# Row standard deviations of an 8192 x 8192 matrix: the last 2048 rows laid out 16 to a partition, and the first group loaded by one transfer

## Chip, cores and metric

The kernel runs on one core of a Trainium2 chip. The metric is the device time of an execution in microseconds (us); before the change its median over three runs is 651.74 us (651.38 to 651.85).

## What is computed

```
x: float32 [8192, 8192], normal random numbers
np.std(x, axis=1)        # float32 [8192]
```

For each row, the root of the mean square deviation from its mean. The input is 268 MB and is read once; the result is 32 KB.

## The kernel before

The 128 partitions P each hold rows of C = 8192 elements (32 KB). 30 groups (G) of 256 rows come first, two neighbouring rows to a partition (64 KB, 8.39 MB in a group), then four tail rows per partition (TR = 4, 4.19 MB each). Three buffers `buf` of one group each are used in turn.

**Loads.** SP issues every load (line 121), in order. Group 0 is loaded by eight transfers of 16 partitions each, `buf[0][k:P:8]` for k = 0 to 7 (lines 124 to 126); all eight increment one semaphore, which is why `landed` (line 108) counts seven more transfers for buffer 0. Groups 1 to 29 are one transfer of 128 partitions each; from group 3 on, SP first waits for the semaphore `free`, which PE's queue increments (line 200) when DVE and ACT are both done with the group that had the buffer. The four tail rows follow: two rows into buffer `xa`, the next in two halves into `xb`, and the last in eight pieces that get shorter (3072 down to 256 elements) into the rest of `xb`.

**Groups 0 to 28.** DVE sums both rows in one instruction (line 161, `s_all`). ACT squares and accumulates each row (line 167 in a loop, `q_all`). DVE turns them into N times the variance, `vN` (lines 250 to 252).

**Group 29 and the tail rows.** A row is split (`shared`, line 214): ACT takes its first 3072 elements with two passes (square, and copy, each with an accumulated sum), DVE takes the rest with `bn_stats` in pieces of 512 (line 206) and aggregates them (line 212). For group 29 DVE joins the two halves (lines 260 to 268); for tail rows POOL does (`joined`, line 227).

**Results.** `vN` is transposed by PE (line 275) so that each group's 256 results lie in one partition, ACT takes roots from PSUM (line 279, `std_g`) and SP stores them (line 282). Three of the tail rows are joined by POOL into `t3`, transposed by PE (line 303), rooted by ACT (line 314) and stored (line 316). The last row's pieces go through ACT, POOL and DVE into `tri`; DVE aggregates them into `fin` (line 318), transposes `fin` in blocks of 32 x 32 (line 320), ACT takes the root (line 322) and SP stores four partitions of 128 bytes (line 324). Then SP waits for the three stores.

The order on each engine is written out by hand; `Line.need` is a wait for another engine's count, `Line.did` an increment.

Of the kernel before, what the change touches and what calls it, by code (L numbers as in the profile page):

```python
# [7 lines left out]
FP32 = mybir.dt.float32  # L8
ACTF = mybir.ActivationFunctionType
# [6 lines left out]
def kernel(  # L16
# [7 lines left out]
    nc = tc.nc  # L24
    P = nc.NUM_PARTITIONS
    R, C = x.shape
    N = float(C)
# [2 lines left out]
    AX = mybir.AxisListType.X  # L30


    TR = 4
    G = (R // P - TR) // 2
    B0 = 2 * (G - 1)
    T0 = 2 * G * P
    xg = x[0:T0, :].rearrange("(g p j) m -> g p (j m)", g=G, p=P, j=2)
    xt_rows = x[T0:R, :].rearrange("(t p) m -> t p m", p=P)
    out_g = out[0:T0].rearrange("(g q) -> g q", q=2 * P)
    out_t = out[T0:R].rearrange("(t p) -> t p", p=P)  # L40

    out_l = out[T0:T0 + P].rearrange("(b i) -> b i", b=4)
    ACT_ROW = 3072
    N_D = float(C - ACT_ROW)
    H = C // 2
    pieces = [(3072, 768), (1536, 1024), (1024, 0), (1024, 512), (512, 0), (512, 0), (256, 0), (256, 0)]

    def sb(name, shape, dt=FP32):
        return ctx.enter_context(nc.sbuf_tensor(name, shape, dt))[:]

    def sem(name):
        return ctx.enter_context(nc.semaphore(name))

    NBUF = 3
    buf = [sb(f"x{i}", [P, 2 * C]) for i in range(NBUF)]

    dump = sb("dump", [P, C], mybir.dt.uint8)
    s_all = sb("s_all", [P, 2 * G + TR])
    q_all = sb("q_all", [P, 2 * G + TR])
    half = sb("half", [P, 2])  # L60
    agg = sb("agg", [P, 2 * G + TR - 1 - B0, 2])
    ident = sb("ident", [P, P])
    cinv = sb("cinv", [P, 1])
    nd = sb("nd", [P, 1])
    vN = sb("vN", [P, 2 * G])
    m2 = sb("m2", [P, 2 * G])
    u, w, uq, wq = (sb(n, [P, TR]) for n in ("u", "w", "uq", "wq"))
    t3 = sb("t3", [P, TR - 1])
    warm = sb("warm", [P, 1])

    fin = sb("fin", [P, 33])
    tr = sb("tr", [P, 32])
    std_l = sb("std_l", [P, 32])
    std_t = sb("std_t", [TR - 1, P])
    std_g = sb("std_g", [G, P, 2])
    n_act = sum(1 for _, a in pieces if a)
    n_bn = sum(-(-(n - a) // F) for n, a in pieces)
    tri = sb("tri", [P, 3 * n_act + n_bn * SD])
    q_p = sb("q_p", [P, n_act])
    m_p = sb("m_p", [P, n_act])  # L80
    bns = [sb(f"bn{i}", [P, (C - ACT_ROW) // F * SD]) for i in range(2)]
    ps_t = ctx.enter_context(nc.psum_tensor("ps_t", [TR - 1, P], FP32))[:]
    ps_g = ctx.enter_context(nc.psum_tensor("ps_g", [G, 2, P], FP32))[:]


    class Line:
# [11 lines left out]
    V = Line(nc.vector, "v")  # L98
    A = Line(nc.scalar, "a")
    Q = Line(nc.gpsimd, "q")  # L100
    T = Line(nc.tensor, "t")
    free, token, row_done, squared = sem("free"), sem("token"), sem("row_done"), sem("squared")
    lane = [sem(f"lane{i}") for i in range(NBUF)]
    NT = 4 + len(pieces)
    tail = [sem(f"tail{i}") for i in range(NT)]
    done_g, done_t, done_l = sem("done_g"), sem("done_t"), sem("done_l")

    def landed(g):
        return lane[g % NBUF], 16 * (g // NBUF + 1 + (P // 16 - 1) * (g % NBUF == 0))

    xl, xa, xb = (buf[k % NBUF] for k in (G - 1, G, G + 1))

# [7 lines left out]
    def load(dst, src, s):  # L120
        nc.sync.dma_start(out=dst, in_=src).then_inc(s, 16)  # L121


    S0 = P // 16
    for k in range(S0):
        load(buf[0][k:P:S0], xg[0][k:P:S0], lane[0])
    for g in range(1, G):
        if g >= NBUF:
            nc.sync.wait_ge(free, g - NBUF + 1)
        load(buf[g % NBUF], xg[g], lane[g % NBUF])  # L130
    nc.sync.wait_ge(free, G - NBUF + 1)
    for i, t in enumerate((1, 2)):
        load(xa[:, i * C:(i + 1) * C], xt_rows[t], tail[i])
    nc.sync.wait_ge(free, G - NBUF + 2)
    for h in range(2):
        load(xb[:, h * H:(h + 1) * H], xt_rows[3][:, h * H:(h + 1) * H], tail[2 + h])
    c0 = 0
    for i, (n, _) in enumerate(pieces):
        load(xb[:, C + c0:C + c0 + n], xt_rows[0][:, c0:c0 + n], tail[4 + i])
        c0 += n  # L140


    def q_op(op, *args, **kw):
        Q.need(Q, Q.n)
        return Q.did(op(*args, **kw))  # L145
# [6 lines left out]
    Q.did(nc.gpsimd.memset(nd, N_D))  # L152
    for j, a in enumerate(a for _, a in pieces if a):
        Q.did(nc.gpsimd.memset(tri[:, 3 * j:3 * j + 1], float(a)))
    Q.did(nc.gpsimd.memset(fin, 0.0))


    v_group = []
    for g in range(G - 1):
        nc.vector.wait_ge(*landed(g))  # L160
        v_group.append(V.did(nc.vector.reduce_sum(  # L161
            out=s_all[:, 2 * g:2 * g + 2],
            in_=buf[g % NBUF].rearrange("p (j m) -> p j m", j=2), axis=AX)))
# [39 lines left out]
    def bn_cols(bn, k, src):  # L203
        n = src.shape[1]
        for d0 in range(0, n, F):
            V.did(nc.vector.bn_stats(out=bn[:, k * SD:(k + 1) * SD], in_=src[:, d0:min(n, d0 + F)]))  # L206
            k += 1
        return k

    def aggregated(out_ap, bn):  # L210
        V.need(V, V.n)
        return V.did(nc.vector.bn_aggr(out=out_ap, in_=bn))  # L212

    def shared(r, parts):
        bn = bns[r % 2]
        k = 0
        for i, (src, arrived) in enumerate(parts):
# [6 lines left out]
            k = bn_cols(bn, k, src[:, a:src.shape[1]])  # L224
        aggregated(agg[:, r - B0, :], bn)

    def joined(out_ap, r0, r1):
        n = r1 - r0
        ndb = nd.to_broadcast((P, n))
        cb = cinv.to_broadcast((P, n))  # L230
        dm, dv = agg[:, r0 - B0:r1 - B0, 0], agg[:, r0 - B0:r1 - B0, 1]
        u_, w_ = uq[:, 0:n], wq[:, 0:n]
        q_op(nc.gpsimd.tensor_mul, u_, dm, dm)
        q_op(nc.gpsimd.tensor_add, u_, u_, dv)
        q_op(nc.gpsimd.tensor_mul, u_, u_, ndb)
        q_op(nc.gpsimd.tensor_add, u_, u_, q_all[:, r0:r1])
        q_op(nc.gpsimd.tensor_mul, w_, dm, ndb)
        q_op(nc.gpsimd.tensor_add, w_, w_, s_all[:, r0:r1])
        q_op(nc.gpsimd.tensor_mul, w_, w_, w_)
        q_op(nc.gpsimd.tensor_mul, w_, w_, cb)  # L240
        return q_op(nc.gpsimd.tensor_sub, out_ap, u_, w_)

    def v_op(op, *args, **kw):
        V.need(V, V.n)
        return V.did(op(*args, **kw))  # L245
# [3 lines left out]
    V.need(A, a_groups)  # L249
    v_op(nc.vector.scalar_tensor_tensor, out=m2[:, 0:B0], in0=s_all[:, 0:B0], scalar=1.0 / N,  # L250
         in1=s_all[:, 0:B0], op0=ALU.mult, op1=ALU.mult)
    v_op(nc.vector.tensor_sub, vN[:, 0:B0], q_all[:, 0:B0], m2[:, 0:B0])
    shared(B0, [(xl[:, 0:C], last)])
# [14 lines left out]
    v_groups = v_op(nc.vector.tensor_sub, vN[:, B0:2 * G], u_, w_)  # L268


    vg = vN.rearrange("p (g j) -> p g j", j=2)
    T.need(V, v_groups)
    T.need(Q, q_ident)
    for j in range(2):
# [3 lines left out]
    for j in range(2):  # L278
        a_std = A.did(nc.scalar.activation(out=std_g[:, :, j], in_=ps_g[:, j, :], func=ACTF.Sqrt,  # L279
                                           scale=1.0 / N))  # L280
    nc.sync.wait_ge(A.sem, a_std)
    nc.sync.dma_start(out=out_g, in_=std_g.rearrange("g p j -> g (p j)")).then_inc(done_g, 16)

    r = 2 * G + 2
# [4 lines left out]
    c0, k, j = C, 0, 0  # L289
    for i, (n, a) in enumerate(pieces):  # L290
        src = xb[:, c0:c0 + n]
        if a:
            cnt, mean, m2v = (tri[:, 3 * j + e:3 * j + e + 1] for e in range(3))
            nc.scalar.wait_ge(tail[4 + i], 16)
            A.did(squash(src[:, 0:a], a, ACTF.Copy, mean, scale=1.0 / a))
            A.did(squash(src[:, 0:a], a, ACTF.Square, q_p[:, j:j + 1]))
            if j == 0:
                Q.need(V, v_blocks)
                Q.need(A, a_blocks)
                q_op(nc.gpsimd.tensor_add, s_all[:, r:r + 1], s_all[:, r:r + 1], half[:, 0:1])  # L300
                q_op(nc.gpsimd.tensor_add, q_all[:, r:r + 1], q_all[:, r:r + 1], half[:, 1:2])
                T.need(Q, joined(t3, 2 * G, r + 1))
                T.did(nc.tensor.transpose(ps_t, t3, ident))  # L303
            Q.need(A, A.n)
            q_op(nc.gpsimd.tensor_mul, m_p[:, j:j + 1], mean, mean)
            q_op(nc.gpsimd.tensor_mul, m_p[:, j:j + 1], m_p[:, j:j + 1], cnt)
            q_op(nc.gpsimd.tensor_sub, m2v, q_p[:, j:j + 1], m_p[:, j:j + 1])
            j += 1
        nc.vector.wait_ge(tail[4 + i], 16)
        k = bn_cols(tri[:, 3 * n_act:], k, src[:, a:n])  # L310
        c0 += n

    A.need(T, T.n)
    a_std = A.did(nc.scalar.activation(out=std_t, in_=ps_t, func=ACTF.Sqrt, scale=1.0 / N))  # L314
    nc.sync.wait_ge(A.sem, a_std)
    nc.sync.dma_start(out=out_t[1:TR], in_=std_t).then_inc(done_t, 16)
    V.need(Q, Q.n)
    aggregated(fin[:, 0:2], tri)
    V.need(V, V.n)
    v_fin = V.did(nc.vector.transpose(out=tr, in_=fin[:, 1:33]))  # L320
    A.need(V, v_fin)
    A.did(nc.scalar.activation(out=std_l, in_=tr, func=ACTF.Sqrt))  # L322
    nc.sync.wait_ge(A.sem, A.n)
    nc.sync.dma_start(out=out_l, in_=std_l[0:P:32, :]).then_inc(done_l, 16)
    nc.sync.wait_ge(done_g, 16)
    nc.sync.wait_ge(done_t, 16)
    nc.sync.wait_ge(done_l, 16)


# [28 lines left out]
```

## Time and profile before

| what | value |
|---|---|
| profiled execution, time | 651.74 us |
| its span on the core | 649.7 us |
| DVE busy | 540.2 us (83% of the span) |
| ACT busy | 450.1 us (69%) |
| PE, POOL busy | 1.0 and 4.8 us |
| moved by DMA | 268.49 MB, 413 GB/s over the span |
| chain that ended last | DMA 62%, DVE 35%, SP's queue 1% |
| SP waits for `free`, in total | 586.3 us, 29 times |
| DVE line 161 waits for loads | 104.2 us, 29 times |

The page divides the span into 40 equal slices and gives for each the busy share of the engines in tenths, the mean busy share of the 16 transfer engines (DMA) and the rate in GB/s. A stage line gives a stretch of time, then each engine's busy time in it, the PE clock, the DMA share and the rate. The chain is followed back from the last instruction, at each step to what released it. In the timeline a row is start, duration, engine, line, operation, output <- input, and in brackets the idle time before it and what ended it. Times are us from the start of the span.

### The profile page before, as it was taken

How to read it: one execution, taken by the hardware profiler on the slowest of the kernel's cores; microseconds unless marked ns; L12 is line 12 of the kernel's file. 1: busy time of each engine (PE TensorE's matmuls, PEld its weight loads, DVE VectorE, ACT ScalarE, POOL GpSimd, SP SyncE). 2: the span in 40 equal slices, each digit the busy share in tenths (PEclk: the TensorE clock that was granted, in tenths of full speed). 3: DMA queues.
4: the chain of work that ended last, by engine and by line, in shares of the span. 5: the costliest groups of instructions: out<-in, count | busy, mean ns of one | idle time of the engine just before them, and what ended most of it. 6: DMA issues, size and time to landing. Idle time of an engine off the chain costs nothing.

```text
span 649.7 us, 684 instructions
## 1 busy us (share of the span) xinstructions
PE 1.0 (0%) x3; PEld 0.2 (0%) x3; DVE 540.2 (83%) x107; ACT 450.1 (69%) x158; POOL 4.8 (1%) x33
## 2 busy tenths in 40 slices
PE   0000000000000000000000000000000000000000
PEld 0000000000000000000000000000000000000000
DVE  0028988888998888998888898888898888899897
ACT  0026886666787666787666687666688666778786
POOL 0000000000000000000000000000000000000002
DMA  9999999999999999999999999999999999999996
GB/s 195 198 307 399 452 452 391 448 452 440 399 452 452 391 448 452 440 399 452 452 391 448 452 440 399 452 452 395 444 452 444 395 452 452 395 444 452 414 417 269
DMA packets 6221, 268.49 MB, mean 413 GB/s; under 512 B 810, under 2 KB 1099, under 8 KB 1739
## 3 DMA queue, kind: packets, MB, share of 16 engines
q1 hardware_dynamic: 6219, 268.47, 99.0%
q14 instruction: 2, 0.02, 0.0%
HBM read 268.44 MB, written 0.03 MB: 413 GB/s over the span
## 4 chain that ended last, share of the span: by engine, by line
DMA 62%; DVE 35%; SPq 1%; another core or an unknown queue 1%; issue 0%; PEldq 0%; ACT 0%; DVEq 0%; POOLq 0%
DMA x<-in_x_dram 62%; DVE s_all L161 29%; DVE bn L206 5%; DVE tri L206 1%; SPq L121 1%; DVE agg L212 0%; PEldq L200 0%; DVE fin L212 0%; DVE u L245 0%; ACT std_l L322 0%; DVE tr L320 0%; DVE w L245 0%; DVE vN L245 0%; DVE w L264 0%
## 5 line engine op out<-in xcount | busy, mean ns | idle before, releaser
L161 DVE TENSOR_REDUCE s_all<-x 128x2 f32<-128x16384 f32 x29 | 499.4, 17220 | 104.2 <-DMA x<-in_x_dram 104.2
L167 ACT ACTIVATE dump<-x 128x8192 uint8<-128x8192 f32 (+5 forms) x76 | 440.8, 5800 | 193.4 <-ACTq L175 169.3
L206 DVE BATCH_NORM_STATS2 bn<-x 128x6 f32<-128x512 f32 x50 | 30.0, 674 | 1.5 <-DMA x<-in_x_dram 1.5
L167 ACT ACTIVATION_READ_ACCUMULATOR dump<-x (+1 forms) x76 | 14.2, 186 | 0.0
L206 DVE BATCH_NORM_STATS2 tri<-x 128x6 f32<-128x512 f32 (+1 forms) x13 | 7.1, 614 | 0.0
L145 POOL TENSOR_TENSOR s_all<-s_all,half 128x1 f32<-128x1 f32 x1 | 0.2, 193 | 636.9 <-DVE agg L212 636.9
L212 DVE BATCH_NORM_AGGREGATE agg<-bn 128x2 f32<-128x60 f32 x5 | 2.1, 425 | 0.2
L171 ACT ACT_TABLE_LOAD x1 | 1.3, 1283 | 1.4 <-PEq L342 1.4
L322 ACT ACTIVATE std_l<-tr 128x32 f32<-128x32 f32 x1 | 0.2, 229 | 2.0 <-DVE tr L320 2.0
L275 PE MATMUL ps_g<-ident,vN 128*30 128x128 f32 x2 | 0.6, 407 | 626.0 <-DVE vN L245 626.0
L212 DVE BATCH_NORM_AGGREGATE fin<-tri 128x2 f32<-128x87 f32 x1 | 0.5, 547 | 0.1
L145 POOL TENSOR_TENSOR m_p<-tri 128x1 f32<-128x1 f32 x3 | 0.6, 194 | 1.4 <-ACT dump L167 1.3
L145 POOL TENSOR_TENSOR m_p<-m_p,tri 128x1 f32<-128x1 f32 x3 | 0.6, 192 | 0.2
L145 POOL TENSOR_TENSOR tri<-q_p,m_p 128x1 f32<-128x1 f32 x3 | 0.6, 192 | 0.2
L279 ACT ACTIVATE std_g<-ps_g 30x128 f32<-30x128 f32 x2 | 0.4, 258 | 0.0
L303 PE MATMUL ps_t<-ident,t 128*3 128x128 f32 x1 | 0.4, 375 | 15.1 <-POOL t L145 15.1
L275 PEld LDWEIGHTS ps_g<-ident,vN 128*30 128x30 f32 x2 | 0.1, 114 | 626.0 <-DVE vN L245 626.0
L245 DVE SCALAR_TENSOR_TENSOR m<-s_all 128x58 f32<-128x58 f32 x1 | 0.2, 220 | 0.1
L145 POOL TENSOR_SCALAR_AFFINE_SELECT ident<-ident 128x128 f32<-128x128 f32 x1 | 0.3, 294 | 0.1
L314 ACT ACTIVATE std_t<-ps_t 3x128 f32<-3x128 f32 x1 | 0.2, 250 | 0.0
L245 DVE TENSOR_TENSOR vN<-q_all,m 128x58 f32<-128x58 f32 x1 | 0.2, 220 | 0.0
L245 DVE TENSOR_TENSOR u<-agg 128x2 f32<-128x2 f32 x1 | 0.2, 160 | 0.1
(28 smaller groups left out, 4.4 us busy)
## 6 DMA issues: line engine op xcount, KB each, us to landing
x<-in_x_dram SPq DMA_DIRECT2D x2, 4096.0 KB, 35.7
x<-in_x_dram SPq DMA_DIRECT2D x2, 2048.0 KB, 28.6
x<-in_x_dram SPq DMA_DIRECT2D x1, 1536.0 KB, 34.0
x<-in_x_dram SPq DMA_DIRECT2D x2, 512.0 KB, 36.7
x<-in_x_dram SPq DMA_DIRECT2D x1, 768.0 KB, 35.5
x<-in_x_dram SPq DMA_DIRECT2D x37, 40.7
x<-in_x_dram SPq DMA_DIRECT2D x2, 256.0 KB, 37.4
x<-in_x_dram SPq DMA_DIRECT2D x2, 128.0 KB, 27.0
```

The source lines that it names most:

```text
L121: nc.sync.dma_start(out=dst, in_=src).then_inc(s, 16)
L145: return Q.did(op(*args, **kw))
L161: v_group.append(V.did(nc.vector.reduce_sum(out=s_all[:, 2 * g:2 * g + 2], in_=buf[g % NBUF].rearrange("p (j m) -> p j m", j=2), axis=AX)))
L167: return nc.scalar.activation(out=dump[:, 0:n], in_=src, func=func, scale=scale, accum_out=acc)
L171: A.did(nc.scalar.activation(out=warm, in_=warm, func=ACTF.Sqrt))
L206: V.did(nc.vector.bn_stats(out=bn[:, k * SD:(k + 1) * SD], in_=src[:, d0:min(n, d0 + F)]))
L212: return V.did(nc.vector.bn_aggr(out=out_ap, in_=bn))
L245: return V.did(op(*args, **kw))
L275: T.did(nc.tensor.transpose(ps_g[:, j, :], vg[:, :, j], ident))
L279: a_std = A.did(nc.scalar.activation(out=std_g[:, :, j], in_=ps_g[:, j, :], func=ACTF.Sqrt, scale=1.0 / N))
L303: T.did(nc.tensor.transpose(ps_t, t3, ident))
L314: a_std = A.did(nc.scalar.activation(out=std_t, in_=ps_t, func=ACTF.Sqrt, scale=1.0 / N))
```

## The change

The last 16 x 128 = 2048 rows are assigned to partitions differently: partition p gets the 16 neighbouring rows 6144 + 16p to 6144 + 16p + 15. The first 24 groups (GA) are as before. Groups 24 to 29 and the four tail rows are now columns of `xe`, the view of those 2048 rows with 16 rows to a partition: each group still has two neighbouring rows (64 KB) to a partition, but from one partition to the next it is 512 KB in x. The number, order and size of the transfers of groups 1 to 29 and of the tail stay.

The results of these 16 rows per partition are rooted in place into `std_e` (128 x 16) by three ACT instructions (12, 3 and 1 columns), and one store at the end writes 64 bytes of each partition. PE's transpose of the tail rows, DVE's transpose, two stores' buffers and the memset of `fin` go. PE's transposes for the groups have 24 columns instead of 30.

Group 0 is loaded by one transfer of 128 partitions, as the other groups are.

```diff
+    E = 16
     G = (R // P - TR) // 2
+    GA = (R // P - E) // 2
-    T0 = 2 * G * P
-    xg = x[0:T0, :].rearrange("(g p j) m -> g p (j m)", g=G, p=P, j=2)
-    xt_rows = x[T0:R, :].rearrange("(t p) m -> t p m", p=P)
+    T0 = 2 * GA * P
+    xg = x[0:T0, :].rearrange("(g p j) m -> g p (j m)", g=GA, p=P, j=2)
+    xe = x[T0:R, :].rearrange("(p e) m -> p (e m)", p=P)
+    xg = [xg[g] for g in range(GA)] + [xe[:, 2 * k * C:2 * (k + 1) * C] for k in range(G - GA)]
+    xt_rows = [xe[:, (E - TR + t) * C:(E - TR + t + 1) * C] for t in range(TR)]
...
-    S0 = P // 16
-    for k in range(S0):
-        load(buf[0][k:P:S0], xg[0][k:P:S0], lane[0])
-    for g in range(1, G):
+    for g in range(G):
...
-    Q.did(nc.gpsimd.memset(fin, 0.0))
...
+    A.did(nc.scalar.activation(out=std_e[:, 0:E - TR], in_=vN[:, 2 * GA:2 * G], func=ACTF.Sqrt,
+                               scale=1.0 / N))
...
-                T.need(Q, joined(t3, 2 * G, r + 1))
-                T.did(nc.tensor.transpose(ps_t, t3, ident))
+                q_t3 = joined(t3, 2 * G, r + 1)
...
-    A.need(T, T.n)
-    a_std = A.did(nc.scalar.activation(out=std_t, in_=ps_t, func=ACTF.Sqrt, scale=1.0 / N))
-    nc.sync.wait_ge(A.sem, a_std)
-    nc.sync.dma_start(out=out_t[1:TR], in_=std_t).then_inc(done_t, 16)
+    A.need(Q, q_t3)
+    A.did(nc.scalar.activation(out=std_e[:, E - TR:E - 1], in_=t3, func=ACTF.Sqrt, scale=1.0 / N))
     V.need(Q, Q.n)
-    aggregated(fin[:, 0:2], tri)
-    V.need(V, V.n)
-    v_fin = V.did(nc.vector.transpose(out=tr, in_=fin[:, 1:33]))
+    v_fin = aggregated(fin, tri)
     A.need(V, v_fin)
-    A.did(nc.scalar.activation(out=std_l, in_=tr, func=ACTF.Sqrt))
+    A.did(nc.scalar.activation(out=std_e[:, E - 1:E], in_=fin[:, 1:2], func=ACTF.Sqrt))
     nc.sync.wait_ge(A.sem, A.n)
-    nc.sync.dma_start(out=out_l, in_=std_l[0:P:32, :]).then_inc(done_l, 16)
+    nc.sync.dma_start(out=out_e, in_=std_e).then_inc(done_e, 16)
```

More of the change, by code (lines that the diff above doesn't have):

```diff
@@ L33 @@
     TR = 4
+    E = 16
     G = (R // P - TR) // 2
+    GA = (R // P - E) // 2
     B0 = 2 * (G - 1)
-    T0 = 2 * G * P
-    xg = x[0:T0, :].rearrange("(g p j) m -> g p (j m)", g=G, p=P, j=2)
-    xt_rows = x[T0:R, :].rearrange("(t p) m -> t p m", p=P)
+    T0 = 2 * GA * P
[3 more added lines that the diff above has]
+    xt_rows = [xe[:, (E - TR + t) * C:(E - TR + t + 1) * C] for t in range(TR)]
     out_g = out[0:T0].rearrange("(g q) -> g q", q=2 * P)
-    out_t = out[T0:R].rearrange("(t p) -> t p", p=P)
-    out_l = out[T0:T0 + P].rearrange("(b i) -> b i", b=4)
+    out_e = out[T0:R].rearrange("(p e) -> p e", p=P)
     ACT_ROW = 3072
@@ L69 @@
     warm = sb("warm", [P, 1])
[L71 to L75, printed above, removed]
+    fin = sb("fin", [P, 2])
+    std_e = sb("std_e", [P, E])
+    std_g = sb("std_g", [GA, P, 2])
     n_act = sum(1 for _, a in pieces if a)
@@ L81 @@
     bns = [sb(f"bn{i}", [P, (C - ACT_ROW) // F * SD]) for i in range(2)]
-    ps_t = ctx.enter_context(nc.psum_tensor("ps_t", [TR - 1, P], FP32))[:]
-    ps_g = ctx.enter_context(nc.psum_tensor("ps_g", [G, 2, P], FP32))[:]
+    ps_g = ctx.enter_context(nc.psum_tensor("ps_g", [GA, 2, P], FP32))[:]
     class Line:
@@ L105 @@
     tail = [sem(f"tail{i}") for i in range(NT)]
-    done_g, done_t, done_l = sem("done_g"), sem("done_t"), sem("done_l")
+    done_g, done_e = sem("done_g"), sem("done_e")
     def landed(g):
-        return lane[g % NBUF], 16 * (g // NBUF + 1 + (P // 16 - 1) * (g % NBUF == 0))
+        return lane[g % NBUF], 16 * (g // NBUF + 1)
     xl, xa, xb = (buf[k % NBUF] for k in (G - 1, G, G + 1))
@@ L131 @@
     nc.sync.wait_ge(free, G - NBUF + 1)
-    for i, t in enumerate((1, 2)):
+    for i, t in enumerate((0, 1)):
         load(xa[:, i * C:(i + 1) * C], xt_rows[t], tail[i])
@@ L135 @@
     for h in range(2):
-        load(xb[:, h * H:(h + 1) * H], xt_rows[3][:, h * H:(h + 1) * H], tail[2 + h])
+        load(xb[:, h * H:(h + 1) * H], xt_rows[2][:, h * H:(h + 1) * H], tail[2 + h])
     c0 = 0
     for i, (n, _) in enumerate(pieces):
-        load(xb[:, C + c0:C + c0 + n], xt_rows[0][:, c0:c0 + n], tail[4 + i])
+        load(xb[:, C + c0:C + c0 + n], xt_rows[3][:, c0:c0 + n], tail[4 + i])
         c0 += n
@@ L268 @@
     v_groups = v_op(nc.vector.tensor_sub, vN[:, B0:2 * G], u_, w_)
-    vg = vN.rearrange("p (g j) -> p g j", j=2)
+    vg = vN[:, 0:2 * GA].rearrange("p (g j) -> p g j", j=2)
     T.need(V, v_groups)
@@ L311 @@
         c0 += n
-    A.need(T, T.n)
-    a_std = A.did(nc.scalar.activation(out=std_t, in_=ps_t, func=ACTF.Sqrt, scale=1.0 / N))
-    nc.sync.wait_ge(A.sem, a_std)
-    nc.sync.dma_start(out=out_t[1:TR], in_=std_t).then_inc(done_t, 16)
+    A.need(Q, q_t3)
+    A.did(nc.scalar.activation(out=std_e[:, E - TR:E - 1], in_=t3, func=ACTF.Sqrt, scale=1.0 / N))
     V.need(Q, Q.n)
-    aggregated(fin[:, 0:2], tri)
-    V.need(V, V.n)
-    v_fin = V.did(nc.vector.transpose(out=tr, in_=fin[:, 1:33]))
+    v_fin = aggregated(fin, tri)
     A.need(V, v_fin)
-    A.did(nc.scalar.activation(out=std_l, in_=tr, func=ACTF.Sqrt))
+    A.did(nc.scalar.activation(out=std_e[:, E - 1:E], in_=fin[:, 1:2], func=ACTF.Sqrt))
     nc.sync.wait_ge(A.sem, A.n)
-    nc.sync.dma_start(out=out_l, in_=std_l[0:P:32, :]).then_inc(done_l, 16)
+    nc.sync.dma_start(out=out_e, in_=std_e).then_inc(done_e, 16)
     nc.sync.wait_ge(done_g, 16)
-    nc.sync.wait_ge(done_t, 16)
-    nc.sync.wait_ge(done_l, 16)
+    nc.sync.wait_ge(done_e, 16)
 _INS = ['x']
```

## The prediction

> **What bounds the kernel now.** I read the page's line of GB/s first, then the stages, then the chain that ended last, then the end of the timeline.
>
> Page, DMA share and GB/s of 40 slices of 16.24 us each:
>
> ```profile
> DMA  9999999999999999999999999999999999999996
> GB/s 195 198 307 399 452 452 391 448 452 440 399 452 452 391 448 452 440 399 452 452 391 448 452 440 399 452 452 395 444 452 444 395 452 452 395 444 452 414 417 269
> ```
>
> The transfer engines are never idle, so the kernel is bound by transfers; but the first two and a half slices move under half of what the others move. Stages (us, engines' busy time, PE clock, DMA share, GB/s):
>
> ```profile
> 3.00:43.00 40.00, 0.00 (x0) 0.00 (x0) 0.00 (x0) 0.00 (x0) 0.00 (x0) 1.00 0.97 205
> 65.00:82.00 17.00, 0.00 (x0) 0.00 (x0) 16.07 (x1) 13.36 (x4) 0.00 (x0) 1.00 1.00 432
> 100.00:605.00 505.00, 0.00 (x0) 0.00 (x0) 448.56 (x29) 370.37 (x104) 0.00 (x0) 1.00 1.00 433
> ```
>
> 205 GB/s until 43 us, then 433 GB/s for the whole middle, at a full DMA share in both. The chain (start, us, what) says what the slow stretch is:
>
> ```profile
> 5.53 39.13 DMA x<-in_x_dram
> 44.66 0.02 issue
> 44.69 17.22 DVE s_all L161
> 61.91 1.92 another core or an unknown queue
> ...
> 83.16 0.02 issue
> 83.19 17.23 DVE s_all L161
> ```
>
> Group 0 lands at 44.66, group 1 at 63.82 (61.91 + 1.92), group 2 at 83.16. The later two take 19.2 and 19.3 us for 8.39 MB each. Group 0 is of the same size and takes 42. In the trace's packet records its 128 packets of 64 KB take 5.11 us (median), eight rounds on 16 transfer engines from 2.36 to 43.74, and every later 64 KB packet 2.42. In the middle, a group lands each 19.35 us while DVE needs 17.22 and ACT 14.5 for it (two passes of 7.03 and their small steps), so DVE and ACT wait for data.
>
> The end:
>
> ```profile
> 638.63 7.09 DVE L206 BATCH_NORM_STATS2 tri<-x 128x6 f32<-128x512 f32 x13
> ...
> 645.83 0.55 DVE L212 BATCH_NORM_AGGREGATE fin<-tri 128x2 f32<-128x87 f32 x1
> 646.41 0.21 DVE L320 STREAM_TRANSPOSE tr<-fin 128x32 f32<-128x32 f32 x1
> 646.65 0.23 ACT L322 ACTIVATE std_l<-tr 128x32 f32<-128x32 f32 x1 [1.99 <-DVE tr L320]
> 646.91 0.60 SPq L324 DMA_DIRECT2D out_dram<-std_l  x1
> ```
>
> From group 29's landing (605.64) DVE runs without a gap to 645.73; the last load lands at 645.05, so DVE and the loads end nearly together. Then a short serial chain: aggregate, transpose, root, store. The profiled execution took 651.74 us, its span 649.7, so 2.04 lie around it; the median of the runs is the same 651.74, and no correction is needed.
>
> **The change, part by part.**
>
> *Group 0 as one transfer.* Eight issues become one. The seven that go (0.57 to 0.72 us each on SP, between 1.63 and 5.49) cost nothing today, since packets flow from 2.36 on, after the first issue; groups 1 and 2 are merely issued 4 us sooner into a queue that has work. What counts is the shape. Each old transfer takes every eighth partition, one 64 KB packet for each transfer engine; the new one is that of groups 1 to 23, whose packets take 2.42. So packets for three groups need 25.17 MB / 433 GB/s = 58.1 us from a start of 2.4 to 3.4 (the first packets of the 16 transfer engines), and 0.4 more to the landing (group 1's last packet ends at 63.4, it lands at 63.82): group 2 lands at 60.9 to 61.9 instead of 83.16, 21.3 to 22.3 earlier. The same per transfer engine: the excess of its first nine packets over 2.42 adds up to 21.2 to 21.9. I take 21.6. The gain passes on: group 3's issue waits for group 0's DVE pass (lands near 23, done near 40), while groups 1 and 2 keep the queue busy to 61.5; the issue comes some 2 us before group 1 lands, as today (61.91 against 63.82). From there each group is as late as the DMA rate makes it, 19.35 us, and all that follows moves by 21.6.
>
> The cause of the 5.11 is not itself in the trace. [...]
>
> *Groups 24 to 29 and the four last rows read another part of x.* 50.3 + 16.8 = 67.1 MB, a quarter of the input, comes in transfers of the same number, size and SBUF side; but neighbouring partitions lie 512 KB apart in x instead of 64 KB (groups) or 32 KB (rows). No such 128-partition load is in this trace. Bounds: nothing, as all packets from 64 KB to 16 KB run at the same rate today (2.42, 1.22, 0.61 us); at the other end, group 0's rate, as its 16 simultaneous rows also lie 512 KB apart: 67.1 / 205 - 67.1 / 433 = 327 - 155 = +172 us. A gain is excluded, since the middle's DMA share is 1.00 at the rate of the shape. I take nothing, the end nearest to the rows with the same SBUF side, and keep the other as a rival.
>
> [...]
>
> *Groups' results.* The two PE transposes narrow from 30 to 24 columns and the two roots keep 128 columns: nothing. One more root on ACT, 128x12, between 0.20 (128x1, line 171) and 0.23 (128x32). Behind it in ACT's queue is the pass over row 2's first half; ACT later waits 0.44 and 0.50 us for loads (634.88, 638.57), which hides it. Without that cover it would delay POOL's last product (645.31, of which DVE's aggregate waits), which has 0.4 us before DVE is ready. Nothing.
>
> *Three tail rows.* PE transpose, root from PSUM and store go; a 128x3 root stays and waits for POOL's result (641.7) where ACT arrives at 644.4: no new stall, and nothing queued behind it but the last root. SP loses one issue (0.26, 644.69) and a wait that ended at 645.82, both before the last store. POOL's dropped memset (0.13 at 1.77) lies in idle time. All nothing.
>
> *Last step.* DVE's transpose goes (0.21 and 0.03 to 0.05 of waits), the root narrows from 0.23 to about 0.20: -0.27. The last store has 128 packets of 64 bytes, eight on each transfer engine, instead of four of 128 bytes. Packets took 11 ns at 128 bytes and 46 at 1 KB, so 8 x 11 - 11 = +0.08 up to 8 x 46 - 11 = +0.36; below, an issue as short as the three-row store's 0.26 instead of 0.60 would give -0.34. I take +0.08, from the nearest size.
>
> Sum: -21.6 - 0.27 + 0.08 = -21.8, so 651.74 - 21.8 = 629.9; I say 630.0.
>
> **Rivals.**
>
> *Row pitch, the slower side.* If HBM gives rows 512 KB apart less than the fabric takes, groups 24 to 29 land later each time. The gain is eaten when 67.1 MB take 154.9 + 21.8 us, that is below 380 GB/s; at 205 GB/s the time is 651.7 - 21.8 + 172 = 802. For it: group 0 fits it just as well, as its simultaneous rows were 512 KB apart. Against: the full-rate groups also read 16 rows at power-of-two distances, and it needs a loss of over 12%. A mild form, 2 to 20 us lost (rates of 428 to 383), gives 632 to 650.
>
> *The slow start isn't the shape.* If the memory or the fabric starts slowly whatever is loaded, group 0 keeps its 42 us and only -0.2 is left: 651.5. For it: by the packet records all 16 transfer engines pass to the faster rate at one instant, about 44.3 (worked out from the start and length of the packet in which each changes), not one by one as they leave group 0 between 42.2 and 43.7; and semaphore packets take 18 ns before and 9 after. Against: that instant is that of group 0's landing (44.3 to 44.7), which a start-up time would meet only by chance.
>
> *The tail becomes the bound*: should loads run ahead, DVE's unbroken 40.1 us from group 29's landing still ends the kernel. It is already so, and moves with the landing.
>
> **How the numbers follow.** Full gain, no pitch loss: 0.62, 628.8 to 631.5. Gain with a mild pitch loss, 632 to 650: 0.15. Pitch loss over 22 us, slower: 0.13. Slow start stays: 0.10, 651 to 652.5. The likeliest gives 630.0. The first two hold 0.77, so the range also takes in the unchanged start: 628.5 to 652.5 leaves out 0.13, the strong pitch loss up to its bound of 802. About 0.2% (1.3 us) is what a measurement of this kernel can tell from no change. Faster by more: 0.77; within: 0.09 (most of the slow start); slower: 0.14.
>
> **What would show it.** Right: group 0 lands near 23 us, its packets at 2.42; the first slices show over 400 GB/s; group 29 lands near 584; landings stay 19.35 apart past group 24; the last store starts about 0.27 sooner after the aggregate. Wrong: 205 GB/s again to 44 us (slow start), or a break at the landing of group 24, with 64 KB packets above 2.42 from there on (pitch). A last store that lands over 0.4 us later after its issue would show the 64-byte packets.

## The result and the profile after

The changed kernel takes 630.45 us (median of 4 runs, 630.36 to 630.78) against 651.62 for the kernel before: ratio 0.9676, 95% interval 0.9659 to 0.9693. The forecast was 630.0, with a range of 628.5 to 652.5. The profiled execution took 630.48 us, its span 628.3: 21.4 less than before.

The page's DMA share and GB/s, now in slices of 15.71 us:

```profile
DMA  9999999999999999999999999999999999999996
GB/s 397 405 463 405 463 405 463 405 463 405 463 405 463 405 463 405 463 405 463 405 463 405 463 405 463 405 463 405 463 405 463 405 459 409 459 409 459 403 414 262
```

The first slices have about the rate of the others; the slow stretch is gone. By stages (columns as before; groups 24 to 29 are on their way from 465 on):

```profile
3.00:22.00 19.00, 0.00 (x0) 0.00 (x0) 0.00 (x0) 0.00 (x0) 0.00 (x0) 1.00 0.92 397
45.00:62.00 17.00, 0.00 (x0) 0.00 (x0) 15.19 (x1) 12.48 (x4) 0.00 (x0) 1.00 1.00 432
...
465.00:583.00 118.00, 0.00 (x0) 0.00 (x0) 105.10 (x8) 85.47 (x24) 0.00 (x0) 1.00 0.99 429
```

397 GB/s where there were 205. The groups read 512 KB apart come at 429, their 64 KB packets keep the median of 2.42 us, and they land 19.35 us apart as before. The timeline's first pass and its end:

```profile
23.62 17.22 DVE L157 TENSOR_REDUCE s_all<-x 128x2 f32<-128x16384 f32 x1 [23.62 <-DMA x<-in_x_dram]
...
624.93 0.55 DVE L208 BATCH_NORM_AGGREGATE fin<-tri 128x2 f32<-128x87 f32 x1
625.51 0.20 ACT L315 ACTIVATE std_e<-fin 128x1 f32<-128x1 f32 x1 [1.79 <-DVE fin L208]
625.74 0.37 SPq L317 DMA_DIRECT2D out_dram<-std_e  x1
```

Group 0 lands at 23.59 instead of 44.66. From there the old rhythm holds; the chain (start, us, what) shows it up to group 29's landing at 584.76:

```profile
42.98 17.22 DVE s_all L157
60.19 2.10 another core or an unknown queue
62.30 0.02 issue
62.32 17.23 DVE s_all L157
...
544.07 40.69 DMA x<-in_x_dram
584.76 0.02 issue
```

The 21.4 us of the span come in three parts: group 29 lands 20.87 sooner (605.64 to 584.77), the way from there to the last store is 0.30 shorter (41.27 to 40.97), and from that store to the end of the span 0.21 (2.80 to 2.59; the 0.23 of the expectations below comes from spans rounded to 0.1).

### The profile page after: what moved, and what is told of

The parts are those of the page before. It is cut to its first block, busy times and chain, and to the rows that moved or that the text cites. A ratio compares the mean times of both kernels' runs of the same rounds, so it can differ in the third digit from the quotient of the medians.

```text
span 628.3 us, 673 instructions
## 1 busy us (share of the span) xinstructions
PE 0.6 (0%) x2; PEld 0.1 (0%) x2; DVE 540.0 (86%) x106; ACT 450.1 (72%) x159; POOL 4.7 (1%) x32
## 4 chain that ended last, share of the span: by engine, by line
DMA 65%; DVE 34%; another core or an unknown queue 0%; issue 0%; PEldq 0%; SPq 0%; ACT 0%; DVEq 0%; POOLq 0%
DMA x<-in_x_dram 65%; DVE s_all L157 27%; DVE bn L202 5%; DVE tri L202 1%; DVE agg L208 0%; PEldq L196 0%; DVE fin L208 0%; DVE u L241 0%; SPq L122 0%; ACT std_e L315 0%; DVE w L241 0%; DVE vN L241 0%; DVE w L260 0%; DVEq L97 0%
```

## The experiments

Theory, a guess of the author's: the eight transfers of group 0 were slow because of the 16 partitions that they address at one time, which would share paths into SBUF (no trace shows paths). Rivals: the 16 rows read at one time lie 512 KB apart in memory; a slow start that passes by itself; the new layout of the last rows is part of the gain.

### Only group 0's load, and the layout alone

`one_old_rows` is the kernel before with

```diff
-    for k in range(S0):
-        load(buf[0][k:P:S0], xg[0][k:P:S0], lane[0])
-    for g in range(1, G):
+    for g in range(G):
```

> The kernel before with one edit: group 0 by one transfer of 128 partitions; the old layout of the last rows, the transposes and the three stores stay. If the gain is that of group 0's load alone: group 0 lands at 23.6 us, group 29 at 584.8, and the time is 651.62 less the 20.87 by which group 29 landed sooner, 630.75; the kernel after then keeps 0.5 us of its own from the shorter end (0.30 between group 29's landing and the last store, 0.23 from the store to the end). Rival: the new layout of the rows is needed for the gain, and the time stays near 651.

`after_again` ran beside it.

> The kernel after, unchanged, beside the three others on one chip: 630.45, 0.3 to 0.5 us below the kernel before with only group 0's load changed.

`eight_new_rows` is the opposite: the kernel after with the old eight transfers.

> The kernel after with the old load of group 0: eight transfers of 16 partitions, every eighth partition in each. With this and the run that changed only group 0's load, the change is split in two. If the slow start belongs to the eight transfers: 64 KB packets of 5.1 us until 44 us, group 0 lands at 44.7, and the time is 630.5 + 21.1 = 651.6 less 0.3 to 0.5 for the shorter end, 651.1 to 651.3. Rival: the new rows help the load by themselves, and the time is below 650.

Measured: `one_old_rows` 630.87 us (630.72 to 631.3), `after_again` 630.51 (630.34 to 630.98), `eight_new_rows` 651.2 (650.99 to 651.4). The ratios to the kernel before are 0.9684 (0.9671 to 0.9697), 0.968 (0.9667 to 0.9693) and 0.9993 (0.9984 to 1.0003). So the whole gain is the load of group 0. The layout, with its dropped transposes and stores, shows 0.36 to 0.37 us in the medians of both pairs (630.87 - 630.51, 651.57 - 651.2), which the interval of `eight_new_rows` can't tell from nothing. The traces show it more sharply: from group 29's landing to the end of the span are 44.06 and 44.05 us with the old layout (the kernel before, `one_old_rows`) and 43.55 to 43.59 with the new one (the kernel after, `after_again`, `eight_new_rows`).

### Which side of the transfer is slow

`eight_src_together` is the kernel before with `xg[0][16 * k:16 * k + 16]` as the source and the same destinations.

> The kernel before, but each of the eight transfers of group 0 reads 16 neighbouring 64 KB runs of x (1 MB in one piece) into every eighth partition, instead of 16 runs that lie 512 KB apart; group 0's results come out in another order of rows. If the side of SBUF makes the packets slow: still 5.1 us for a packet and 651.5. Rival, the distance in memory does it: 2.42 us for a packet and 630.8. In one_old_rows that distance isn't separated from the SBUF side.

Measured: 651.58 us. This and the next four kernels, `eight_blocks`, `two_halves`, `four_strided` and `eight_at_12`, were executed once each at first; what is read from them is 20 us and more, while repeated runs of the kernels before and after lie within 0.9 us. The stage of group 0:

```profile
3.00:43.00 40.00, 0.00 (x0) 0.00 (x0) 0.00 (x0) 0.00 (x0) 0.00 (x0) 1.00 0.97 205
```

The same 205 GB/s and 5.11 us for a packet with the source in one piece: distance in memory isn't the cause of group 0's rate. `eight_blocks` keeps source and result as before and takes neighbours:

```diff
-        load(buf[0][k:P:S0], xg[0][k:P:S0], lane[0])
+        load(buf[0][16 * k:16 * k + 16], xg[0][16 * k:16 * k + 16], lane[0])
```

> The kernel before, but each of the eight transfers of group 0 covers 16 neighbouring partitions (and 16 neighbouring runs of x) instead of every eighth. [...] In numbers of the theory alone: if a block of 16 neighbours reaches half as many paths as every eighth partition, packets take 10.2 us, group 0 lands near 85 and the time is 651.5 + 41 = 692. Rival, a transfer of only 16 partitions is slow whichever they are: 5.1 us and 651.5. Rival, distance in memory: 2.42 us and 630.8.

Measured: 685.81 us, group 0 landed at 78.61. Its stage, and group 1's:

```profile
3.00:78.00 75.00, 0.00 (x0) 0.00 (x0) 0.00 (x0) 0.00 (x0) 0.00 (x0) 1.00 0.93 112
82.00:97.00 15.00, 0.00 (x0) 0.00 (x0) 13.85 (x1) 11.14 (x4) 0.00 (x0) 1.00 1.00 433
```

112 GB/s with packets of 9.39 us, so the direction of the theory came, with a smaller loss than its 10.2 us and 692. The rate of transfers of 16 partitions depends on which 16: every eighth gives 205 GB/s, about a half of 433, and 16 neighbours 112, about a quarter. Then two ways of covering group 0 in fewer, larger transfers, in the kernel after: `two_halves` (`buf[0][64 * h:64 * h + 64]`, h = 0, 1) and `four_strided`:

```diff
+    for k in range(4):
+        load(buf[0][k:P:4], xg[0][k:P:4], lane[0])
+    for g in range(1, G):
```

> The kernel after with group 0 loaded by two transfers of 64 neighbouring partitions (0 to 63, then 64 to 127). [...] Rival: from 64 partitions on, or with four packets for each transfer engine, all paths are used: 2.42 us and 630.5.

> The kernel after with group 0 loaded by four transfers of every fourth partition (32 each). [...] Rival: what counts is which two of the 32 partitions each transfer engine takes at the same time; if it takes neighbours of the list, the 16 packets in flight are again every eighth partition, and the time is 651.5 as with eight transfers.

Measured: `two_halves` 651.12 us, packets 5.12 us; `four_strided` 630.04, packets 2.42; both rivals failed. Stages 3 to 43 us of the first and 3 to 22 of the second:

```profile
3.00:43.00 40.00, 0.00 (x0) 0.00 (x0) 0.00 (x0) 0.00 (x0) 0.00 (x0) 1.00 0.92 193
```

```profile
3.00:22.00 19.00, 0.00 (x0) 0.00 (x0) 0.00 (x0) 0.00 (x0) 0.00 (x0) 1.00 0.91 393
```

Neither the size of a transfer nor its number of partitions decides: 64 neighbours are slow (193 GB/s) and 32 spread over all 128 are not (393). The rates of the stages measured here are 112 GB/s for 16 neighbours, 205 for every eighth partition, 193 for 64 neighbours (205 by their packets of 5.12 us), 393 for every fourth and 397 for all 128. The runs show that the set of partitions decides; what the partitions of a slow set share, no trace here shows.

### Is it the start?

`eight_at_12`: the kernel after with the eight transfers at group 12.

```diff
-        load(buf[g % NBUF], xg[g], lane[g % NBUF])
+        if g == 12:
+            for k in range(P // 16):
+                load(buf[g % NBUF][k:P:P // 16], xg[g][k:P:P // 16], lane[g % NBUF])
+        else:
+            load(buf[g % NBUF], xg[g], lane[g % NBUF])
```

> The kernel after with group 12, in the middle, loaded by eight transfers of every eighth partition; group 0 by one. If the shape of the transfers is slow wherever it stands: group 12's packets take 5.1 us, it lands 22 us late, DVE and ACT wait for it, and the time is 630.5 + 21 to 22.5 = 651.5 to 653. Rival, a slow start of the memory or the fabric that passes with time: 630.5.

Measured: 652.68 us, 22.2 above the kernel after. Before, within and after the slow group:

```profile
200.00:230.00 30.00, 0.00 (x0) 0.00 (x0) 27.87 (x2) 24.69 (x7) 0.00 (x0) 1.00 0.99 428
232.00:268.00 36.00, 0.00 (x0) 0.00 (x0) 19.60 (x2) 14.24 (x4) 0.00 (x0) 1.00 1.04 233
270.00:300.00 30.00, 0.00 (x0) 0.00 (x0) 19.79 (x2) 16.55 (x5) 0.00 (x0) 1.00 0.95 382
```

The rate falls at group 12 as it did at group 0 (233 and 382 because the edges of the stretches cut packets of both kinds; the slow ones take 5.09). The DMA share stays near 1 (1.04 at 233 GB/s, 0.93 at 112 in `eight_blocks`): a transfer engine counts as busy through a packet of 9.39 us as through one of 2.42.

### The other rival: rows far apart in memory

The kernel after with E = 32, 48 and 64 neighbouring rows to a partition. Only E changes for 32 and 48; with 64 no group is left over, so PE's transposes, their roots and their store go.

> The kernel after with 32 neighbouring rows to a partition in place of 16: 134 MB instead of 67 MB are read with neighbouring partitions 1 MB apart in x. If distance in memory costs a load nothing, 64 KB packets stay at 2.42 us, landings 19.35 us apart, and the time is 630.4. Rival: the distance begins to cost between 512 KB and 1 MB; each per cent of the rate lost over 134 MB adds 3.1 us.

> The kernel after with 48 neighbouring rows to a partition: 201 MB are read with neighbouring partitions 1.5 MB apart. With 1 MB and 134 MB the time was 640.0, with 2 MB and 268 MB 645.3, against 630.5 at 512 KB. If the loss grows with the distance: between 637 and 648. Rival, the power of two in the distance counts, so that the rows read at one time lie alike in memory: 1.5 MB is not one, and the loss is gone or much smaller, 630.4 to 634.

> The kernel after with 64 neighbouring rows to a partition: the whole input is read with neighbouring partitions 2 MB apart; all results go out in one store of 256 bytes of each partition, and the groups' transposes and their store go too. If distance in memory costs a load nothing: 630.2 to 630.5, as what goes is off the path. [...]

| rows to a partition | distance in x | read so | us (runs) | ratio to before, 95% |
|---|---|---|---|---|
| 16 (`after_again`) | 512 KB | 67 MB | 630.51 (630.34 to 630.98) | 0.968 (0.9667 to 0.9693) |
| 32 | 1 MB | 134 MB | 640.0 (636.91 to 642.33) | 0.9815 (0.9789 to 0.9841) |
| 48 | 1.5 MB | 201 MB | 630.5 (630.35 to 630.61) | 0.9677 (0.9661 to 0.9693) |
| 64 | 2 MB | 268 MB | 645.28 (644.94 to 646.06) | 0.9906 (0.9891 to 0.9921) |

My expectation of no loss failed for 32 and 64, and the rival is right that the distance can cost, beyond the case's 512 KB. For 48 the expectation of 637 to 648 failed and its rival came. The loss isn't a steady rate. The stages of `rows32`: 64 KB apart, after the step to 1 MB (group 16 follows at about 314), and later:

```profile
100.00:300.00 200.00, 0.00 (x0) 0.00 (x0) 177.40 (x11) 147.39 (x41) 0.00 (x0) 1.00 1.00 431
312.00:372.00 60.00, 0.00 (x0) 0.00 (x0) 47.99 (x4) 41.54 (x11) 0.00 (x0) 1.00 1.01 389
400.00:580.00 180.00, 0.00 (x0) 0.00 (x0) 159.46 (x10) 132.68 (x37) 0.00 (x0) 1.00 1.00 430
```

`rows48` after its own step to 1.5 MB (group 8 follows at about 159), and in the middle one of the stretches above:

```profile
157.00:217.00 60.00, 0.00 (x0) 0.00 (x0) 51.68 (x4) 42.74 (x12) 0.00 (x0) 1.00 1.01 437
312.00:372.00 60.00, 0.00 (x0) 0.00 (x0) 51.66 (x3) 42.74 (x12) 0.00 (x0) 1.00 1.01 436
```

And `rows64` at its start, in its last groups and in the tail rows (DVE, ACT and POOL, then clock, DMA share, GB/s):

```profile
3.00:60.00 57.00, 28.91 (x2) 25.47 (x7) 0.00 (x0) 1.00 0.98 395
...
500.00:580.00 80.00, 71.47 (x5) 59.83 (x17) 0.00 (x0) 1.00 1.00 433
...
625.00:635.00 10.00, 6.19 (x11) 4.99 (x9) 2.71 (x14) 1.00 0.95 221
```

So the length of the distance doesn't order the loss: 1 and 2 MB cost time, 512 KB and 1.5 MB nothing. Whether it is a power of two from 1 MB on or a multiple of 1 MB that counts, these four can't tell. In the trace of `rows32` most of the loss comes just after the pattern begins: of the 10 us by which group 29 lands later than in the kernel after, the first four groups of the pattern make 8.5; later it runs at 430. In that of `rows64` the first five groups lose 7.4 us, group 29 lands 9.7 late, and another 5.6 us are lost in the tail rows, whose smaller packets run at 221 GB/s for a while. The recovery is shown, its reason isn't, nor is that of the loss in the tail. The runs of `rows32` scatter by 5.4 us, also without a shown cause. In the medians 2 MB cost 14.8 us against `after_again`.

### Every fourth partition, timed

`four_strided` had landed group 0 at 23.11 instead of 23.59 and was timed as `four_timed`.

> The kernel after with group 0 by four transfers of every fourth partition, now timed in rounds: one look gave 630.04 with group 0 landed at 23.11 instead of 23.59 us. If the 0.5 us by which the groups land sooner is kept: 630.0, under every run of the kernel after (630.34 to 630.98). Rival: the one look was a good draw, and the median is 630.4 to 630.5.

Measured: 630.22 us (630.14 to 630.25), ratio 0.9673 (0.966 to 0.9686). In its trace group 0 lands at 23.29 and group 29 at 584.46, 0.31 sooner than in the kernel after and 0.19 sooner than in `after_again`; no transfer engine has the second packet of 2.95 us that makes one of them late in both of those (2.44 at most). All five runs lie under the nine of the kernel after and its repeat, so about half of the hoped 0.5 us came; but the 0.2 to 0.3 us are smaller than the ratio's interval, and the runs were made on another chip than `after_again`. That this version is faster is not shown.

## Why the prediction was right, step by step

- **Group 0 as one transfer, -21.6.** Right in mechanism and place, a little too large: group 0 landed 21.07 sooner, group 29 20.87. The sum had priced all of the new transfer's packets at 2.42; the first one of each of the 16 transfer engines took 2.58 to 3.61 (over an engine's eight packets of group 0 the excess is 0.75 us in the mean). The first packets also began about 0.5 us sooner than before (1.96 to 2.90 instead of 2.36 to 3.43), which the sum did not count; but group 0 landed (23.59) 0.47 after the last of its packets ended (23.12), and that one was on the engine whose first two packets took 3.47 and 2.95, 1.60 us over the price (the other engines were done with theirs by 22.66).
- **The cause** was left open between the SBUF side and distance in memory, and the chance of the second kept the range wide. `eight_src_together`, `eight_blocks`, `two_halves` and `four_strided` settle it for the SBUF side, that is for the set of partitions written (112 to 393 GB/s by the set, 205 with either source), `eight_at_12` against the start. What a slow set shares was not shown.
- **Groups 24 to 29 and the tail at 512 KB, 0.** Right: landings stay at 19.35 us past group 24 and packets at 2.42. There was luck in it: no row of the kernel before could tell it, and at twice the distance, with twice the bytes, the same choice would have failed by 10 us (`rows32`).
- **The slow start** (0.10) is refuted by the profile after itself and by `eight_at_12`. Its evidence was a misreading: that all 16 transfer engines change speed at one instant is no sign of a start-up time. In `eight_blocks` they change together too, at 78.2 by the same reckoning, 0.4 before group 0's landing (78.61), as 44.3 is 0.4 before 44.66. The semaphore packets' 18 ns come back in `eight_at_12` while group 12 loads, with 9 after it. Both go with the transfers.
- **Results, three tail rows: nothing.** Right: ACT's extra 128x12 root took 0.196 us, and its waits for loads at 614.00 and 617.70 (0.35 and 0.51) still follow.
- **Last step, -0.27 + 0.08.** The first part came as -0.30 between landing and store. The second had the wrong sign: the store of 128 x 64 bytes issues in 0.37 us instead of 0.60 and lands 1.44 after the start of its issue instead of 1.62; the packets take 8 to 11 ns. Store to end gave -0.21, within the bounds (-0.34 to +0.36). The term that moved is the issue, which the prediction had only as its lower bound; the choice by the nearest packet size left it out.

Sum: -20.87 - 0.30 - 0.21 = -21.4, predicted -21.8. It came this close partly by luck: group 0's term was 0.7 too large and the last step's 0.3 too small, and the two errors partly cancel.

## What to carry to other kernels

Look at the rate in GB/s, not at the busy share of the transfer engines: group 0 held them at a share of 0.97 with 205 GB/s when its transfers took every eighth partition, and of 0.93 with 112 when they took 16 neighbours, against 433 in the middle. So cut a load along the free dimension (the tail's halves, 16 KB to a partition, take 0.615 us a packet here, 426 GB/s on 16 engines, nearly the 433 of the 64 KB packets), or take every fourth partition (393 GB/s from the start of the kernel, where one transfer of all 128 has 397); 64 neighbours were slow here too (193). When a change bundles a layout with a transfer shape, split it: here the new layout of 2048 rows was worth 0.4 to 0.5 us and the one transfer for group 0 21. Distances of 1 and 2 MB in x between neighbouring partitions cost 10 and 15 us here, 512 KB and 1.5 MB nothing.

## What was not expected

- The 16 transfer engines recover all together: in `eight_blocks` the first packets of group 1 took 4.78 for the engine that began at 75.05 and 3.29 for the one that began at 77.08, both consistent with one change at 78.2. Why packets of group 1 that have already begun stay slow until then is open.
- The slow rates aren't exact fractions of 433: 205 is less than a half (217), 112 more than a quarter (108).
- A store of 64 bytes from each of 128 partitions issues faster (0.37 us) than one of 128 bytes from 4 (0.60), while one of 512 bytes from 3 took 0.26; `one_old_rows`, which keeps the four-partition store, still has the 0.60.
